# Tiles that matmuls read at multiples of 128 bytes, and the first u tiles loaded over half of h, in a hybrid attention block

## The chip, the cores and the metric

The kernel runs on one core of a Trainium2 chip. The metric is the device time in microseconds (us). All times are of single executions; the profile is one execution, taken with the hardware profiler. The engines are TensorE (PE: matmuls; PEld: its weight loads), VectorE (DVE), ScalarE (ACT), GpSimd (POOL) and SyncE (SP). SP and POOL issue nearly all DMAs, each in the order of its own queue.

## What is computed

One decoder layer for 512 tokens of width 2048, in float32, with three gated branches:

```
h    = rms_norm(x) * g                                    # 512 x 2048
proj = h @ w_in                                           # 2048 x 13712, split into the parts below
A: indexer scores -> causal top-128 of the keys -> grouped-query attention with a relative-position bias
B: latent attention (low-rank q and kv, rotary part), causal and dense, 8 heads
C: cross-attention into 256 memory tokens, 4 heads (k, v = rms_norm(mem) @ w_mem_kv)
u_n  = o_n * silu(z_n)                    for n in A, B, C      # 512 x 1024 each
y    = sum_n sigmoid(gate_n) * (u_n @ w_branch[n])              # 512 x 2048
out  = x + y @ w_out
```

## The kernel before

**Precision and matmuls.** Every large product runs as three matmuls. Each operand is split into a high and a low half (`split`, L257): ACT rounds the high half, DVE subtracts to get the low half. High times high and the two cross products are added up in PSUM. Weights become the tiles `whi` and `wlo`, h becomes `hh0..hh3` and `hl0..hl3` (four tiles of four 128-row blocks each), the gated branch outputs become `u`. Most matmuls have 512 columns.

**The weight stream.** `stream` (L310) is one list of chunks that PE follows in order. SP loads weights in pieces of 256 x 512 into `wraw` (three buffers, `NRAW`) and `sraw`; each is split two to three jobs ahead (`LOOK`), and a piece is loaded as soon as the splitting of an older one has freed its buffer. A job of a plain chunk is two 128-row blocks: 2 x 4 x 3 matmuls with 512 columns, or 12 in a job of Strassen's scheme. The order of the chunks:
1. the memory tokens' k and v;
2. the index queries;
3. Strassen products (`strassen_chunk`, L1495) for the queries of C, the latents and the gates: here weights stream over h, or over the sums `hS1, hS2, hS4` of quarters of h;
4. the rest of the input projection, among it the gated chunks (`gated_chunk`, L796), in which h streams over the weights;
5. `branch_chunk` (L1623), three times four, weights over u, in the order C, B, A;
6. `out_chunk` (L1692), weights over the merged rows `mh, ml`.

**Threads.** The attentions, norms and transposes are generators beside that stream. `run` (L510) steps a thread when a planner (`Plan`, L73) believes its inputs ready: the planner keeps a clock for each engine from fixed prices, 0.422 ns a column plus 11 ns for such a matmul. The order on each engine is so written out when the kernel is built. A thread can also wait for a flag that another part sets. Every instruction passes through `Plan.call` (L139), so nearly all rows of the profile carry L139, and groups are told apart by their tiles.

**How u is loaded.** The last gated chunk is the second half of branch B. Its `post` is `close_h` (L1761): the pool of h is closed, the pool `bp` is opened in its place on the right side of the memory, and the flag "z end" is set. `u_thread` (L1585) waits for that flag, then takes the four u tiles of branch C from `bp` (they lie where hh0, hl0, hh1 and hl1 lay) and loads them from DRAM by GpSimd's queue. In that queue they stand behind the stores of the last gated halves (`sp_u<-zo`, `sp_u<-zs`), which wait for PE, ACT and DVE. The u tiles of branch B follow one by one, each after its tile's last use by branch C ("u2 out k"); those of branch A are made on the core.

**Where tiles start.** `Slots` (L153) hands out tiles from pools; a tile takes its size rounded up to 32 bytes per partition, one after the other. Pools on the left grow upward. The first tile, `ident`, starts at 4,224 = 33 x 128. The constants' pool `cp` then holds 5,280 = 41 x 128 + 32 bytes, so the next pool, `wp` with wraw, whi and wlo, starts at 9,504, which is 32 above a multiple of 128. The other left pools carry that 32 on: memory tokens, hS, the latents, `mh`, `ml`, and most tiles of branch B's attention. The right side ends at 229,344 = 1,791 x 128 + 96, so h, u, yg and ym start 96 above a multiple. In between small tiles shift it: branch C's halves (`c_qh`, `c_kh`, `c_ph`) start at 96, branch A's `a_kh`, `a0_qh` at 64, and the bf16 table `tab` of branch A (93,568) at 0. `mnegb` (bf16, 6,048) starts at 32. `ident` at 0 is the moving operand of the transposes.

The functions of the diff and what calls them:

Of the kernel before, what the change touches and what calls it, by code (L numbers as in the profile page):

```python
# [10 lines left out]
F32 = mybir.dt.float32  # L11
F32R = mybir.dt.float32r
BF = mybir.dt.bfloat16
# [7 lines left out]
P = 128  # L21
T = 512
# [26 lines left out]
    return c  # L49


PE = object()
PRODUCTS = ("P1", "P2", "P3", "P4", "P5", "P6", "P7")


class Engine:
# [3 lines left out]
    def __init__(self, plan, eng, kind):  # L60
        self._plan, self._eng, self._kind = plan, eng, kind
# [11 lines left out]
class Plan:  # L73
# [72 lines left out]
    def ready(self, waits, slack, slack_pe):  # L146

        t = max([x.next_free() if isinstance(x, Ring) else self.done(x.tensor.name, self.wrote)
                 for x in waits if x is not PE], default=0.0)
        return t + (slack_pe if any(x is PE or isinstance(x, Ring) for x in waits) else slack)  # L150


class Slots:  # L153


    def __init__(self, plan, pool):
        self.plan, self.pool, self.past = plan, pool, {}

    def free(self, tag, n):
        past = self.past.get(tag, ())  # L160
# [3 lines left out]

    def tile(self, shape, dt, name, tag=None, bufs=1):
        tag = tag or name
        t = self.pool.tile(shape, dt, name=name, tag=tag, bufs=bufs)
        self.plan.read[t.tensor.name] = {"slot": self.free(tag, bufs)}
        self.past.setdefault(tag, []).append(t.tensor.name)
        return t  # L170
# [60 lines left out]
class Kern:  # L231
# [6 lines left out]


    @contextmanager  # L240
    def slots(self, name, **k):
        with self.tc.tile_pool(name=name, bufs=1, **k) as p:
            yield Slots(self.plan, p)

    def rsqrt(self, pool, y, v, n):

# [316 lines left out]
    def setup(self):  # L563
        nc, A = self.nc, self.A
        cp = self.cp
        jp = self.wp.tile([P, 2, 512], I32, name="jp", tag="ev", bufs=4)[:, 0, :P]
        nc.gpsimd.iota(jp, pattern=[[1, P]], base=0, channel_multiplier=-1)
        self.ident = cp.tile([P, P], F32, name="ident")
        warm = cp.tile([P, 1], F32, name="warm")
        nc.vector.memset(warm, 0.0)  # L570
        nc.scalar.activation(warm, warm, AF.Copy)
        nc.vector.tensor_scalar(self.ident, jp, 0.0, None, op0=OP.is_equal)
        self.identb = cp.tile([P, P], BF, name="identb")
        nc.vector.tensor_scalar(self.identb, jp, 0.0, None, op0=OP.is_equal)
        self.mneg = cp.tile([P, P], F32, name="mneg")
        nc.vector.tensor_scalar(self.mneg, jp, 0.0, NEG, op0=OP.is_gt, op1=OP.mult)
        self.mlow = cp.tile([P, P], F32, name="mlow")
        nc.vector.tensor_scalar(self.mlow, jp, 0.0, LOW, op0=OP.is_gt, op1=OP.mult)
        self.mnegb = cp.tile([P, P], BF, name="mnegb")
        nc.vector.tensor_copy(self.mnegb, self.mneg)  # L580
# [215 lines left out]
    def gated_chunk(self, n, c):  # L796

        nc = self.nc
        dt = self.sp["u%d%d" % (n, c)] = self.dp.tile([P, 2, 4, 512], F32, name="sp_u")
        key = "ABC"[n]  # L800
        box = {}
        new = lambda name: self.wp.tile([P, 2, 512], F32, name=name, tag="ev", bufs=4)

        def act(k):
            if k == 8:
                box["o"] = [new("zo") for _ in range(2)]
                for h, o in enumerate(box["o"]):
                    nc.gpsimd.dma_start(o, self.sp["o%s%d" % (key, c)][:, 2 * h:2 * h + 2])
            return self.act_h(k)

        def evac(b, p):
            if b % 2 == 0:
                box["s"] = new("zs")
            st, o = box["s"], box["o"][b // 2]
            s = st[:, b % 2]
            nc.scalar.activation(s, p, AF.Tanh, scale=0.5)
            nc.vector.scalar_tensor_tensor(s, s, 1.0, p, op0=OP.add, op1=OP.mult)
            if b % 2 == 0:
                return

            def gated():
                nc.vector.scalar_tensor_tensor(st, st, 0.5, o, op0=OP.mult, op1=OP.mult)

            def halves():
                h, l = o.bitcast(F32R), st.bitcast(F32R)
                self.split(h, l, st)
                nc.gpsimd.dma_start(dt[:, 0, b - 1:b + 1], o)
                nc.gpsimd.dma_start(dt[:, 1, b - 1:b + 1], st)
            self.defer(gated, False, 2)
            self.defer(halves, b == 3, 1)  # L830
        col = (AZ, BZ, CZ)[n] + c * 512
        self.chunk(self.A["w_in"][0, :, col:col + 512], KT, 512, act, "fm", 4, evac,
                   lambda k: (key if n != 1 or c else "B heads") if k == 8 else None)

# [747 lines left out]
                            lambda i, j: self.sp[keys[j]][:, 2 * i:2 * i + 2], None, done)  # L1582


    def u_thread(self):  # L1585

        nc = self.nc
        self.u = {}
        yield "z end"
        for n in (2, 1):  # L1590
            self.u[n] = []
            for k in range(4):
                if n == 1:
                    yield "u2 out %d" % k
                u = self.bp.tile([P, 2, 2, 512], F32R, name="u", tag="u", bufs=4)
                self.u[n].append(u)
                c, b = divmod(2 * k, 4)
                nc.gpsimd.dma_start(u.bitcast(F32), self.sp["u%d%d" % (n, c)][:, :, b:b + 2])
                self.flags.add("u%d%d" % (n, k))
        yield "A"  # L1600

        def load(k):
            s, o = [self.bp.tile([P, 2, 512], F32, name="u_" + x, tag="so", bufs=4) for x in "so"]
            c, b = divmod(2 * k, 4)
            nc.gpsimd.dma_start(s, self.sp["s0%d" % c][:, b:b + 2])
            nc.gpsimd.dma_start(o, self.sp["oA%d" % c][:, b:b + 2])
            return s, o
        ahead = [load(0), load(1)]
        self.u[0] = []
        for k in range(4):  # L1610
            s, o = ahead.pop(0)
            yield [s, o]
            nc.vector.scalar_tensor_tensor(s, s, 0.5, o, op0=OP.mult, op1=OP.mult)
            yield "u1 out %d" % k
            u = self.bp.tile([P, 2, 2, 512], F32R, name="u", tag="u", bufs=4)
            self.u[0].append(u)
            yield [s]
            self.split(u[:, 0], u[:, 1], s)
            if k < 2:
                ahead.append(load(k + 2))  # L1620
            self.flags.add("u0%d" % k)
# [93 lines left out]
    def build(self):  # L1715
        ctx, tc, A = self.ctx, self.tc, self.A
        self.flags, self.sp, self.chunks, self.later, self.kept = set(), {}, [], [], []
        self.turn = 0
        pool = lambda n, **k: ctx.enter_context(self.slots(n, **k))
        self.cp = pool("cp")  # L1720
        self.wp = pool("wp")
        hpool = ExitStack()
        self.hp = hpool.enter_context(self.slots("hp", side="right"))
        self.dp = pool("dp", space=DRAM)
        self.pg = Ring(self.plan, ctx.enter_context(tc.tile_pool(name="pg", bufs=4, space=PSUM)), "pg", 4)
        banks = ctx.enter_context(ExitStack())
# [32 lines left out]
            self.flags.add("gates")  # L1759

        def close_h():  # L1761
            hpool.close()
            self.bp = bpool.enter_context(self.slots("bp", side="right", reuse_waits="tile"))
            self.flags.add("z end")

# [10 lines left out]
        self.b_ss = self.cp.tile([P, 8, 8], F32, name="b_ss")  # L1776
        self.c_ss = self.cp.tile([P, 4, 6], F32, name="c_ss")
        self.l_ss = self.cp.tile([P, 3, NT], F32, name="l_ss")
        self.h = [[self.hp.tile([P, 4, T], F32R, name="h%s%d" % (x, q)) for x in "hl"] for q in range(4)]
        self.act_h = lambda k: tuple(x[:, k % 4] for x in self.h[k // 4])  # L1780
        win = A["w_in"][0]
        spool = ExitStack()
# [103 lines left out]
            self.a_bias_thread(), self.a_thread(0), self.a_thread(1), self.h_ops_thread(), self.u_thread()])  # L1886
        tpool.close()
        bpool.close()


@with_exitstack
# [23 lines left out]
```

## Time and profile before

| | us |
|---|---|
| median of 3 runs | 1927.47 (1923.93 to 1927.51) |
| the profiled execution | 1927.66 |
| its span, first to last instruction | 1925.9 |
| PE busy in it | 1887.0 |
| DVE busy | 1315.7 |
| ACT busy | 821.3 |
| POOL busy | 196.3 |

The share of the 16 DMA engines' time is 34.5% for SP's queue and 18.2% for GpSimd's; HBM is read and written at 169 GB/s over the span. The granted clock of PE is 0.995 in the mean.

How to read it: a row of a group is "engine operation out<-moving,stationary, shapes, count | busy us, mean ns of one | idle time before, and what ended it". Matmuls overlap: one lasts some 390 ns from its start to its modelled end, but the next one starts after some 230. The cost of a matmul is therefore read from one start to the next, in the timeline, and not from its duration. Columns of the timeline are start (us from the span's start), length, engine and instruction.

### The profile page before, as it was taken

The page shows a single profiled execution, that of the slowest core. Times are in us where ns is not written, and L with a number is a line of the kernel's source. Part 1 is how long each engine was busy: PE and PEld are TensorE (multiplying, and loading weights), DVE is VectorE, ACT ScalarE, POOL GpSimd, SP SyncE. Part 2 cuts the span into 40 slices and gives each one's busy share as a digit, 9 for nine tenths or more (in the row PEclk, how much of TensorE's full clock was granted, in tenths as well). Part 3 has the DMA queues.
Part 4 walks back from the last instruction along what each step waited for, and adds up shares of the span by engine and source line. Part 5 has one row for each costly group of instructions (what it writes and reads, how often), then busy time and mean ns, then how long its engine had stood idle before and what let it go on. Part 6 is the DMA issues. An engine that isn't in the chain of part 4 may idle for free.

```text
span 1925.9 us, 24974 instructions
## 1 busy us (share of the span) xinstructions
PE 1887.0 (98%) x9437; PEld 1564.0 (81%) x9437; DVE 1315.7 (68%) x2064; ACT 821.3 (43%) x1369; POOL 196.3 (10%) x308
## 2 busy tenths in 40 slices
PE   8999999999999999999999999999969999999999
PEld 6789888888888888889888888788758888778887
DVE  5676877877778768665668799975768965543232
ACT  6643554544444444447666644343323333222111
POOL 1000000000000000112110111002022222110000
PEclk9999999999999999999999999999979999999999
DMA  8754555555555556546643454335465566753442
GB/s 265 245 167 146 162 175 153 171 169 164 164 155 174 165 154 205 170 147 214 211 143 98 150 170 145 112 110 163 135 213 178 193 238 222 274 180 126 143 140 79
DMA packets 142953, 326.82 MB, mean 170 GB/s; under 512 B 13728, under 2 KB 18736, under 8 KB 142576
## 3 DMA queue, kind: packets, MB, share of 16 engines
q1 hardware_dynamic: 108176, 203.58, 34.5%
q0 software_dynamic: 34624, 121.63, 18.2%
q8 instruction: 74, 1.21, 0.3%
q14 instruction: 47, 0.39, 0.1%
q10 hardware_dynamic: 32, 0.01, 0.0%
HBM read 262.49 MB, written 62.69 MB: 169 GB/s over the span
## 4 chain that ended last, share of the span: by engine, by line
PE 92%; DVE 4%; DMA 2%; ACT 1%; issue 1%; POOL 0%; ACTq 0%; DVEq 0%; POOLq 0%
PE pg L139 58%; PE pn L139 24%; PE pb L139 3%; PE pa L139 3%; PE ra L139 2%; DVE wlo L139 1%; PE rb L139 1%; DMA wraw<-w_mem_kv 1%; ACT whi L139 1%; DVE m L139 0%; DMA u<-sp_u 0%; ACT junk L139 0%; DVE yg L139 0%; DVE i_wk L139 0%; DVE i_mx L139 0%
## 5 line engine op out<-in xcount | busy, mean ns | idle before, releaser
L139 DVE TENSOR_TENSOR wlo<-wraw,whi 128x1024 fp32r<-128x1024 f32 (+2 forms) x293 | 354.4, 1210 | 333.6 <-ACT whi L139 330.6
L139 ACT ACTIVATE whi<-wraw 128x1024 fp32r<-128x1024 f32 (+2 forms) x293 | 306.6, 1047 | 527.6 <-PE pg L139 249.1
L139 PE MATMUL pg<-whi,u 128*128 128x512 f32 x640 | 220.3, 404 | 18.7 <-DMA u<-sp_u 17.8
L139 PE MATMUL pg<-hh,whi 128*128 128x512 f32 x512 | 208.3, 407 | 2.0 <-DVE stage L139 1.3
L139 PE MATMUL pg<-hh,wlo 128*128 128x512 f32 x512 | 202.2, 395 | 0.0
L139 PE MATMUL pg<-hl,whi 128*128 128x512 f32 x512 | 202.0, 395 | 0.0
L139 PEld LDWEIGHTS pg<-whi,u 128*128 128x128 f32 x640 | 121.4, 190 | 43.7 <-issue 19.5
L139 PE MATMUL pg<-whi,hh 128*128 128x512 f32 x384 | 152.7, 398 | 0.0
L139 PE MATMUL pg<-wlo,hh 128*128 128x512 f32 x384 | 150.9, 393 | 0.0
L139 PE MATMUL pg<-whi,hl 128*128 128x512 f32 x384 | 149.7, 390 | 0.0
L139 DVE TENSOR_TENSOR wlo<-sraw,whi 128x1024 fp32r<-128x1024 f32 x79 | 96.6, 1225 | 54.4 <-ACT whi L139 54.2
L139 ACT ACTIVATE whi<-sraw 128x1024 fp32r<-128x1024 f32 x79 | 83.4, 1058 | 106.8 <-DVE sraw L139 41.2
L139 PE MATMUL pg<-wlo,u 128*128 128x512 f32 x320 | 126.1, 394 | 0.0
L139 PE MATMUL pn<-whi,hS 128*128 128x512 f32 x384 | 126.0, 389 | 0.0
L139 PE MATMUL pg<-whi,hS 128*128 128x512 f32 x384 | 126.0, 389 | 0.0
L139 PE MATMUL pn<-wlo,hh 128*128 128x512 f32 (+1 forms) x320 | 122.7, 383 | 0.0
L139 PE MATMUL pn<-whi,hh 128*128 128x512 f32 (+1 forms) x320 | 122.4, 383 | 0.0
L139 PE MATMUL pn<-whi,hl 128*128 128x512 f32 (+1 forms) x320 | 121.1, 378 | 0.0
L139 PEld LDWEIGHTS pg<-hh,whi 128*128 128x128 f32 x512 | 96.3, 188 | 23.4 <-DVE stage L139 2.2
L139 PEld LDWEIGHTS pg<-hh,wlo 128*128 128x128 f32 x512 | 96.1, 188 | 23.3
L139 PEld LDWEIGHTS pg<-hl,whi 128*128 128x128 f32 x512 | 96.4, 188 | 19.2
L139 DVE TENSOR_TENSOR wlo<-T,whi 128x1024 fp32r<-128x1024 f32 x64 | 78.2, 1222 | 36.0 <-ACT whi L139 35.8
(422 smaller groups left out, 3888.7 us busy)
## 6 DMA issues: line engine op xcount, KB each, us to landing
wraw<-w_in SPq DMA_DIRECT2D x161, 512.0 KB, 3.7
sraw<-w_in SPq DMA_DIRECT2D x79, 512.0 KB, 3.7
wraw<-w_branch SPq DMA_DIRECT2D x48, 512.0 KB, 4.2
wraw<-w_mem_kv SPq DMA_DIRECT2D x32, 512.0 KB, 5.2
wraw<-w_out SPq DMA_DIRECT2D x32, 512.0 KB, 3.7
yg<-sp_g POOLq DMA_DIRECT2D x24, 512.0 KB, 6.1
u<-sp_u POOLq DMA_DIRECT2D x8, 1024.0 KB, 7.7
sp_m<-yg POOLq DMA_DIRECT2D x16, 512.0 KB, 4.8
```

The costliest lines, as they stand in the source:

```text
L139: return f(*a, **k)
```

## The change

There are two parts.

**Alignment.** `Slots` gets a `line` of 128 bytes, for all pools but those of PSUM, DRAM and the constants. When a tag is taken for the first time, its size (rounded up to 32, times its buffers) is filled up to a multiple of 128 by a pad tile that nothing uses. In `cp`, a tile `rest` of 96 bytes after `ident` moves what follows to the next multiple of 128 for the tiles identb, mnegb and the end of the pool. On the right, a tile `edge` of 96 bytes makes h and what follows it start at a multiple.

**The loads of u.** h is held in two pools, the first for its tiles of blocks 0 to 7 and the second for blocks 8 to 15. Only the second is closed by `close_h`; `bp` opens in its place. The u tiles are taken from the first pool under the tags of hh0, hl0, hh1 and hl1, so that each waits for the readers of that tile only. The flag that starts them, "z half", is set in the last gated chunk before its block 8, that is when its first half has been issued. The four loads of branch C are issued by SP in place of GpSimd; those of branch B stay on GpSimd. The first pool is closed at the end of the kernel.

```diff
 class Slots:
-    def __init__(self, plan, pool):
-        self.plan, self.pool, self.past = plan, pool, {}
+    def __init__(self, plan, pool, line=0):
+        self.plan, self.pool, self.past, self.line = plan, pool, {}, line
...
     def tile(self, shape, dt, name, tag=None, bufs=1):
         tag = tag or name
+        new = tag not in self.past
         t = self.pool.tile(shape, dt, name=name, tag=tag, bufs=bufs)
+        if new and self.line:
+            size = math.prod(shape[1:]) * (2 if dt == BF else 4)
+            rest = -((size + 31) // 32 * 32 * bufs) % self.line
+            if rest:
+                self.pool.tile([P, rest // 4], F32, name="pad_" + tag, tag="pad_" + tag, bufs=1)
...
-    def slots(self, name, **k):
+    def slots(self, name, line=LINE, **k):
         with self.tc.tile_pool(name=name, bufs=1, **k) as p:
-            yield Slots(self.plan, p)
+            yield Slots(self.plan, p, 0 if "space" in k else line)
...
         self.ident = cp.tile([P, P], F32, name="ident")
+        cp.tile([P, 24], F32, name="rest")
...
         def act(k):
+            if k == 8 and n == 1 and c == 1:
+                self.flags.add("z half")
             if k == 8:
...
+    def u_tile(self, k):
+        u = self.hp[0].tile([P, 4, T], F32R, name="u", tag="h%s%d" % ("hl"[k % 2], k // 2))
+        return u.rearrange("p (x k) t -> p x k t", x=2)
...
-        yield "z end"
+        yield "z half"
         for n in (2, 1):
...
-                u = self.bp.tile([P, 2, 2, 512], F32R, name="u", tag="u", bufs=4)
+                u = self.u_tile(k)
...
-                nc.gpsimd.dma_start(u.bitcast(F32), self.sp["u%d%d" % (n, c)][:, :, b:b + 2])
+                (nc.sync if n == 2 else nc.gpsimd).dma_start(u.bitcast(F32), self.sp["u%d%d" % (n, c)][:, :, b:b + 2])
...
-        self.cp = pool("cp")
+        self.cp = pool("cp", line=0)
...
-        hpool = ExitStack()
-        self.hp = hpool.enter_context(self.slots("hp", side="right"))
+        hpool, hpool2 = ExitStack(), ExitStack()
+        edge = ctx.enter_context(self.tc.tile_pool(name="edge", bufs=1, side="right"))
+        edge.tile([P, (LINE - 32) // 4], F32, name="edge")
+        self.hp = [hpool.enter_context(self.slots("hp", side="right")),
+                   hpool2.enter_context(self.slots("hp2", side="right"))]
...
         def close_h():
-            hpool.close()
+            hpool2.close()
             self.bp = bpool.enter_context(self.slots("bp", side="right", reuse_waits="tile"))
             self.flags.add("z end")
...
-        self.h = [[self.hp.tile([P, 4, T], F32R, name="h%s%d" % (x, q)) for x in "hl"] for q in range(4)]
+        self.h = [[self.hp[q // 2].tile([P, 4, T], F32R, name="h%s%d" % (x, q)) for x in "hl"] for q in range(4)]
...
         bpool.close()
+        hpool.close()
```

The u tiles of branch A use `u_tile` in the same way.

More of the change, by code (lines that the diff above doesn't have):

```diff
@@ L49, in constants @@
     return c
+LINE = 128
 PE = object()
@@ L1614, in u_thread @@
             yield "u1 out %d" % k
-            u = self.bp.tile([P, 2, 2, 512], F32R, name="u", tag="u", bufs=4)
+            u = self.u_tile(k)
             self.u[0].append(u)
```

## The prediction

> **What bounds the kernel now.** I read the page first, then who waited for whom, then the rows of TensorE (PE) by shape, and last the PE timeline in a few quiet stretches.
>
> ```profile
> span 1925.9 us, 24974 instructions
> PE 1887.0 (98%) x9437; PEld 1564.0 (81%) x9437; DVE 1315.7 (68%) x2064; ACT 821.3 (43%) x1369; POOL 196.3 (10%) x308
> ```
>
> PE is busy for 98% of the span, so the end moves with two things: the time from one matmul to the next, and the waits of PE. The longest waits are:
>
> ```profile
> PE pg L139 <- DMA u<-sp_u: 17.8, 1, 17.8
> PE pb L139 <- DMA g_rows<-mem_norm_g: 4.6, 1, 4.6
> PE pg L139 <- DVE wlo L139: 2.3, 3, 0.8
> ```
>
> One wait of 17.8 us stands out: the load of u, which the change moves. Its chain, and the stretch around it (columns: PE, PEld, DVE, ACT and POOL busy, granted clock, DMA share, GB/s):
>
> ```profile
> 1398.04 0.55 POOL sp_u L139
> ...
> 1403.30 8.45 DMA u<-sp_u
> ```
> ```profile
> 14.60:110.00 95.40, 92.87 (x431) 75.42 (x432) 61.49 (x94) 61.81 (x104) 9.67 (x15) 1.00 0.75 238
> 190.00:820.00 630.00, 629.26 (x2762) 517.99 (x2761) 477.59 (x457) 297.06 (x372) 29.44 (x43) 1.00 0.54 168
> 1110.00:1270.00 160.00, 157.97 (x784) 129.40 (x783) 147.23 (x319) 66.38 (x111) 15.52 (x26) 1.00 0.43 137
> ...
> 1412.00:1419.00 7.00, 7.00 (x51) 5.49 (x52) 1.93 (x7) 0.77 (x2) 0.00 (x0) 0.61 0.89 348
> ```
>
> GpSimd first stores the four last gated halves (from 1398.04) and then issues the u loads at 1403.30; the first lands 8.45 us later. Behind the wait the granted clock is 0.61 for 7 us, against 1.00 in the stretches without a wait.
>
> Now the pace, from start to start in stretches where PE does nothing else. "Offset" is a tile's start address modulo 128, from the layout given above.
>
> ```profile
> 149.72 0.39 PE L139 MATMUL pg<-hl,whi 128*128 128x512 f32 x1
> ...
> 156.96 0.40 PE L139 MATMUL pg<-hh,wlo 128*128 128x512 f32 x1
> ...
> 701.58 0.39 PE L139 MATMUL pg<-whi,hS 128*128 128x512 f32 x1
> ...
> 704.30 0.39 PE L139 MATMUL pg<-whi,hh 128*128 128x512 f32 x1
> ...
> 709.79 0.39 PE L139 MATMUL pg<-whi,hS 128*128 128x512 f32 x1
> ...
> 1419.40 0.39 PE L139 MATMUL pg<-whi,u 128*128 128x512 f32 x1
> ...
> 1421.91 0.40 PE L139 MATMUL pg<-whi,u 128*128 128x512 f32 x1
> ...
> 1645.83 0.40 PE L139 MATMUL pn<-whi,u 128*128 128x512 f32 x1
> ...
> 1649.80 0.40 PE L139 MATMUL pn<-whi,u 128*128 128x512 f32 x1
> ```
>
> All are matmuls of 512 columns; the first name is the moving operand, the second the stationary one.
> - Both at offset 32 (weights over hS): 12 starts in 2.72 us, 226.7 ns each.
> - Moving at 32, stationary at 96 (weights over hh, hl): 24 in 5.49 us, 228.8 ns. Weights over u, the same offsets: 11 in 2.51 us (228.2 ns) and 17 in 3.97 us (233.5 ns); I take 230.9, the middle.
> - Moving at 96, stationary at 32 (h over weights): 31 in 7.24 us, 233.5 ns.
>
> So the pace goes with the offsets, though the work is the same. No wide matmul here has a moving operand at offset 0. Narrow ones do:
>
> ```profile
> L139 PE MATMUL pg<-wlo,mh 128*128 128x512 f32 x128 | 49.8, 389 | 0.0
> L139 PE MATMUL rb<-tab,a_st 128*128 128x64 bf16 x320 | 23.6, 192 | 0.0
> L139 PE MATMUL rb<-tab,a_st 128*128 128x32 bf16 x320 | 22.7, 178 | 0.0
> L139 PE MATMUL pa<-c_ph,c_vh 128*128 128x256 f32 x32 | 9.0, 282 | 0.0
> L139 PE MATMUL pb<-mnegb,identb 128*128 128x128 bf16 x32 | 7.4, 230 | 0.0
> ```
>
> The duration of one is a constant plus its columns: (389 - 282) / 256 = 0.418 ns a column. What is left is 175 ns for the two f32 rows (offsets 32 and 96) and 176.5 for mnegb (offset 32, bf16), but 165.2 and 164.6 for tab, the one operand here that starts at offset 0. So a moving operand off the 128-byte boundary costs 11.3 ns more, whatever its type. Ends are modelled, so this is a hint and no proof. It fits the pace: 512 columns at 0.418 are 214.0 ns, and 226.7 - 11.3 = 215.4.
>
> **The change part by part.**
>
> *Alignment.* It adds no instruction, only pads. All tiles that PE reads move to offset 0, so both operands have equal offsets. I price an aligned 512-column matmul at 215.4 ns; the bounds are 214.0 (columns alone) and 226.7 (equal offsets help, 0 is not special). I take 215.4 because tab is the nearest row at offset 0. The counts:
>
> ```profile
> L139 PE MATMUL pg<-hh,whi 128*128 128x512 f32 x512 | 208.3, 407 | 2.0 <-DVE stage L139 1.3 <-DVE zs L139 0.7
> L139 PE MATMUL pg<-whi,hh 128*128 128x512 f32 x384 | 152.7, 398 | 0.0
> L139 PE MATMUL pn<-whi,hh 128*128 128x512 f32 x256 | 100.4, 392 | 0.0
> L139 PE MATMUL pn<-whi,hh 128*128 128x400 f32 x64 | 22.1, 345 | 0.0
> ```
> ```profile
> 0.00:1926.00 1926.00, 1561.09 (x4928) 0.99 0.53 170
> ```
> ```profile
> 0.00:1926.00 1926.00, 961.24 (x2464) 0.99 0.53 170
> ```
> ```profile
> 0.00:1926.00 1926.00, 287.28 (x1152) 0.99 0.53 170
> ```
>
> The last three rows (PE busy with its count, clock, DMA share, GB/s) count the matmuls that read whi, wlo and u. Weights: 4928 + 2464 = 7392. Each row with hh stands for three equal ones (hi·hi and the two cross terms).
> - h over weights: 3 x 512 = 1536, x (233.5 - 215.4) = 27.8 us.
> - weights over h: 3 x (384 + 256) = 1920, x 13.4 = 25.7 us.
> - weights over u: 1152, x 15.5 = 17.9 us.
> - the 400-column ones: 3 x 64 = 192, x 11.3 = 2.2 us.
> - the rest, 7392 - 4800 = 2592 (memory tokens, hS, merged rows, latents), x 11.3 = 29.3 us.
> - the attentions' own products of 256 columns and more (c_ph above is one group of many): some 700; between 0 and 8 us, taken at 4, since short bursts among weights are often held by something else.
>
> Sum 106.9 us. The Trainium skill, "TensorE: Matmul & The Clock Gate", section "Back-to-back issue gap", gives N/2.4 + 2.5 ns, 215.7 for 512 columns; no run so far shows it, since the best pace here is 226.7. By it the sum would be some 2 us smaller.
>
> *What takes part of that back.* A faster PE needs the others to follow.
> - 1110 to 1270 us: the top-k selection keeps DVE busy for 147.2 of 160 us. PE would gain 784 x 13 ns = 10 us, down to 150, with DVE left 98% busy. Between 0 and 10 is lost; I take 6, as DVE also needs gaps.
> - 14.6 to 110 us: DMA at 0.75 share, 238 GB/s, feeds the first weights; of 431 x 11.3 ns = 4.9 us I give back 3 (0 to 4.9).
> - 190 to 820 us: DVE 477.6 of 630 us; PE would need about 597. Covered, nothing lost.
> - The order is written for a planner that prices such a matmul at 227 ns; a real 215 shortens every hand-over of the attention chains. 0 to 8 us, taken at 3, because none of them shows a wait now.
>
> Together 12 us back.
>
> *The u loads.* Four loads of 1 MB for branch C leave GpSimd's queue, where they stood behind four stores, and go to SP at the middle of the last gated chunk. The tiles they overwrite are the first half of h, read for the last time before this row:
>
> ```profile
> 1365.12 0.39 PE L139 MATMUL pg<-hh,whi 128*128 128x512 f32 x1
> ...
> 1393.70 0.39 PE L139 MATMUL pg<-hh,wlo 128*128 128x512 f32 x1
> ```
> ```profile
> u<-sp_u POOLq DMA_DIRECT2D x8, 1024.0 KB, 7.7
> ```
>
> From 1365.12 the chunk has 96 of its 192 matmuls left, 28.6 us. Now four loads begin at 1403.30; at the 348 GB/s of the 1412-to-1419 row 4.2 MB take 12 us. So they land some 16 us before they are needed. The 17.8 us go, and with them the low clock: (1 - 0.61) x 7 = 2.7 us. What is late next is the eviction of the chunk's first bank, which runs while its last matmuls do; at most 0.7 us (the zs wait in the hh row above). On SP the wait for PE holds the weight loads queued behind it. Three buffers and two to three split tiles stand ahead of PE then, some 5 jobs of 24 matmuls (28 us at 233.5 ns); the loads behind are late by at most the 12 us. I cost that at 0; without the cover it is 12 us. The loads of branch B stay on GpSimd. Gain 20.5 us.
>
> *Sum.* The profiled execution took 1927.66 us (span 1925.9), 0.2 above the median of 1927.47. 1927.7 - 106.9 + 12 - 20.5 = 1812.3 us. Own range of this case: 1796 (nothing given back, 8 us from the attentions) to 1839 (all 22.9 us of the bounds given back, nothing from the attentions, 12 us on SP).
>
> **The rivals.**
>
> *Only the mismatch is cured.* The 11 ns may belong to 4-byte operands at any offset; then everything runs at 226.7. For it: 226.7 is rigid, and a plain constant explains every width too. Against: mnegb is bf16 and has the 11 ns. Gain 1536 x 6.8 + 1920 x 2.1 + 1152 x 4.2 = 19.3 us, plus 20.5, less 1 for the selection: 1889 us.
>
> *Offsets are not the cause.* The differences could come from which buffers the streams share with other engines' traffic. Then only the u loads count: 1907 us. The Trainium skill, "Advanced Engine Details and Errata", section "Memory Cachelines", gives SBUF lines of 16 bytes; by it 32 and 96 are as good as 0, and this case would hold. The trace speaks against it: 226.7 and 233.5 ns at offsets that are both multiples of 16.
>
> *Slower.* Equal offsets at 0 might be the bad phase: a weight load and a moving read that start on the same line of the same bank. Place: every wide matmul. Price: the slowest pace seen, 233.5, against 229.4 now (the mean of the groups above), over 7200 of them: 29.5 us lost, 20.5 won, 1937 us. It decides from 232.2 ns on. Against: equal offsets at 32 are the fastest of all.
>
> That tiles stay unaligned can be ruled out by adding: the left pools begin 96 bytes higher, at 9,600 = 75 x 128, the right end is 229,248 = 1,791 x 128, and each new tag is padded to 128.
>
> **How the numbers follow.** A measurement of this kernel tells 0.2%, some 4 us, from no change. Forecast (1812): 0.62. Only the mismatch (1889): 0.20. Only the u loads (1907): 0.09. Slower (1937): 0.05. A cancellation within 0.2%: 0.04. So faster 0.91, same 0.04, slower 0.05. The range goes from 1796 to 1892: it holds nearly all of the forecast and of the first rival, about 0.8.
>
> **What would show it.** Weights over hS fall from 226.7 to 215.4 ns from start to start, and h over weights to the same pace; durations at 512 columns fall from 389 to about 378. No u wait in PE's list, no low clock near 1394, u on SP. DVE over 95% busy in the selection, with new PE waits for wlo there. If the pace stops at 226 to 227 in all groups, the step "215.4" is wrong; if the groups still differ, the offsets are not the cause; if PE waits for wlo just before the first branch chunk, SP's queue was held too long.

## The result and the profile after

| | median, us | ratio to before [95% interval] |
|---|---|---|
| before | 1927.49 (1923.93 to 1927.79) | 1 |
| after | 1894.14 (1893.69 to 1894.73) | 0.9831 [0.9814, 0.9848] |

The change saves 33 us, 1.7%. The forecast was 115 us; the measured time lies just above the range, and 5 us from the rival "only the mismatch is cured" (1889). The profiled execution took 1894.73 us.

The first two lines of the page of after, busy time by engine:

```profile
span 1892.9 us, 24971 instructions
PE 1871.0 (99%) x9437; PEld 1561.9 (83%) x9437; DVE 1315.6 (70%) x2064; ACT 820.7 (43%) x1369; POOL 193.5 (10%) x304
```

PE still bounds the kernel. Its busy time has fallen by 16 us and the span by 33, so half of the gain was idle time. The longest waits of PE after (us in total, times, longest):

```profile
PE pb L140 <- DMA g_rows<-mem_norm_g: 4.5, 1, 4.5
PE pn L140 <- DVE m L140: 2.2, 6, 0.8
PE pg L140 <- DVE wlo L140: 2.2, 3, 0.8
```

The 17.8 us for u are gone, and no wait has come in their place. SP's queue shows why (start, length, what it issued):

```profile
1349.98 7.91 SPq L140 DMA_DIRECT2D wraw<-w_branch  x2
1358.07 2.83 SPq L140 DMA_DIRECT2D u<-sp_u  x4
1364.08 34.03 SPq L140 DMA_DIRECT2D wraw<-w_branch  x6
```

The four loads leave at 1358.07, some 25 us before the first matmul needs them. On PE's timeline the last gated matmul and the first of the branch then follow each other without a gap:

```profile
1383.46 0.39 PE L140 MATMUL pg<-hh,wlo 128*128 128x512 f32 x1
1383.69 0.39 PE L140 MATMUL pg<-whi,u 128*128 128x512 f32 x1
```

The granted clock there, and the load of the engines in three other stretches (columns as in the prediction):

```profile
190.00:820.00 630.00, 629.26 (x2777) 520.70 (x2776) 481.88 (x468) 297.78 (x372) 29.44 (x43) 1.00 0.55 170
820.00:1110.00 290.00, 289.29 (x1588) 251.91 (x1587) 199.50 (x419) 183.28 (x473) 43.60 (x67) 1.00 0.49 156
1110.00:1270.00 160.00, 157.55 (x790) 130.76 (x789) 148.91 (x319) 67.59 (x112) 15.52 (x26) 1.00 0.44 139
1383.00:1392.00 9.00, 9.00 (x55) 7.36 (x54) 7.69 (x9) 5.53 (x10) 1.64 (x3) 1.00 0.35 106
```

The clock behind the hand-over is 1.00 where it was 0.61. DVE is 93% busy in the selection (148.91 of 160), not the 98% that a faster PE would have brought. Now the pace, in the longest quiet stretches of PE's timeline: 108 starts of h over weights, then 36 of weights over h.

```profile
1296.68 0.39 PE L140 MATMUL pg<-hh,whi 128*128 128x512 f32 x1
...
1320.94 0.39 PE L140 MATMUL pg<-hh,wlo 128*128 128x512 f32 x1
```
```profile
232.42 0.39 PE L140 MATMUL pn<-whi,hh 128*128 128x512 f32 x1
...
240.35 0.39 PE L140 MATMUL pn<-whi,hl 128*128 128x512 f32 x1
```

24.26 us / 107 = 226.7 ns and 7.93 / 35 = 226.6 ns, against 233.5 and 228.8 before. In such stretches all groups have come to the pace that weights over hS had, and none is faster. Aligned operands do not run at 215.4 ns. The groups (busy us, mean ns of one) say the same of the hint behind that number:

```profile
L140 PE MATMUL pg<-hh,whi 128*128 128x512 f32 x512 | 206.4, 403 | 2.5 <-DVE stage L140 1.7 <-DVE zs L140 0.8
L140 PE MATMUL rb<-tab,a_st 128*128 128x64 bf16 x320 | 23.3, 191 | 0.0
L140 PE MATMUL pb<-mnegb,identb 128*128 128x128 bf16 x32 | 7.4, 230 | 0.0
```

`mnegb` now starts at a multiple of 128 and still takes 230 ns by the profile. The 11 ns by which it stood above `tab` were not its offset.

### The profile page after: what moved, and what is told of

Same layout as the page of the kernel before. It is cut to its first block, busy times and chain, and to the rows that moved or that the text cites. A ratio compares the mean times of both kernels' runs of the same rounds, so it can differ in the third digit from the quotient of the medians.

```text
span 1892.9 us, 24971 instructions
## 1 busy us (share of the span) xinstructions
PE 1871.0 (99%) x9437; PEld 1561.9 (83%) x9437; DVE 1315.6 (70%) x2064; ACT 820.7 (43%) x1369; POOL 193.5 (10%) x304
## 4 chain that ended last, share of the span: by engine, by line
PE 90%; DVE 4%; DMA 3%; ACT 1%; issue 1%; POOL 0%; SPq 0%; ACTq 0%; DVEq 0%; POOLq 0%
PE pg L140 57%; PE pn L140 23%; PE pb L140 3%; PE pa L140 3%; PE ra L140 2%; DVE wlo L140 1%; DMA wraw<-w_mem_kv 1%; DMA ym<-sp_m 1%; PE rb L140 1%; ACT whi L140 1%; DVE m L140 0%; DVE yg L140 0%; ACT junk L140 0%; DMA u_o<-sp_oA 0%; DMA px<-mem 0%
```

## The experiments

The theories, as the expectations use them. A: equal start addresses of the two operands make the wide matmuls faster, and the wait for u is a separate 20 us. B: the addresses do nothing. C: the wait for u shrinks by itself once the rest is faster. D: what counts for u is which queue loads it, not when. E: 0 modulo 128 itself counts, not equality. F: a period of 64 bytes. G: a period longer than 128 bytes, which the change meets by chance.

### The two parts alone

**e_align** keeps the alignment and starts the loads as before:

```diff
-            if k == 8 and n == 1 and c == 1:
-                self.flags.add("z half")
...
-        yield "z half"
+        yield "z end"
...
-                (nc.sync if n == 2 else nc.gpsimd).dma_start(u...
+                nc.gpsimd.dma_start(u...
```

> The changed kernel with the u loads put back to where they were: started by the flag at the end of the last gated chunk and issued by GpSimd; all tiles stay at multiples of 128. Theory A (what counts is that moving and stationary operand have equal offsets, and the wait for u is a separate 20 us): pace 226.7 to 229 ns in all groups, a PE wait of some 18 us for u, 1914 us (1894 + 20). Rival B (the offsets do nothing and the u loads brought all of it): 1927 us, paces as in the kernel before. Rival C (the wait for u shrinks by itself once the pace is faster): under 1905 us.

Measured: 1915.1 us, 0.9939 [0.9924, 0.9954]. The wait for u is back in PE's list:

```profile
PE pg L140 <- DMA u<-sp_u: 17.3, 1, 17.3
```

**e_uload** keeps the early loads and takes the pads away (`LINE = 0`, no `rest`, no `edge`).

> The changed kernel without any pad, so with the offsets of the kernel before (weights 32, h and u 96); only the early u loads on SP remain. Theory A: 1907 to 1909 us (1927.5 less 18 to 20), no PE wait for u, h over weights still at 233.5 ns. Rival B: 1894 us. If the two parts do not add up (their gains differ from 33 us in sum by over 4), something joins them.

Measured: 1905.46 us, 0.9887 [0.9872, 0.9902], and no wait for u. Before took 1926.86 us beside these runs: alignment alone saves 11.8 us, the loads alone 21.4, and both together 33. The parts add up. So neither B nor C holds, and the early loads are worth some 21 us at either pace.

### Queue or place

**e_half_pool** loads u at the new place, but from GpSimd; **e_end_sp** at the old place, but from SP.

```diff
-                (nc.sync if n == 2 else nc.gpsimd).dma_start(u...
+                nc.gpsimd.dma_start(u...        # e_half_pool
```
```diff
-            if k == 8 and n == 1 and c == 1:
-                self.flags.add("z half")
...
-        yield "z half"
+        yield "z end"                           # e_end_sp
```

> The changed kernel with the four u loads of branch C issued by GpSimd, still at the middle of the last gated chunk. Theory A (the earlier place in the order is what counts): 1893 to 1896 us, no PE wait for u. Rival D (the queue counts, GpSimd is held by its stores): a PE wait of 5 to 18 us for u comes back, 1900 to 1914 us.

> The changed kernel with the four u loads on SP, but started at the end of the last gated chunk. Theory A: SP does not stand behind the four stores, but the transfer itself (8.45 us to the first landing) is exposed, and some low clock with it: a PE wait of 8 to 11 us for u, 1903 to 1906 us. Rival D (the queue alone does it): 1894 us.

Measured: 1894.28 us for the place without SP (0.9828 [0.9814, 0.9843]), the same as after; 1910.9 us for SP without the place (0.9918 [0.9901, 0.9934]), with 14.1 us of waiting, more than the 8 to 11 us and 1906 us that I expected at most. The wait of e_end_sp, and its chain (start, length), which shows what I had missed:

```profile
PE pg L140 <- DMA u<-sp_u: 14.1, 1, 14.1
```
```profile
1385.16 1.22 DVE zs L140
1386.37 1.15 DVE wlo L140
...
1387.54 0.37 SPq L140
...
1388.08 9.64 DMA u<-sp_u
```

SP's queue is no free road at that place. A weight load stands at its head; it waits for the buffer that DVE frees with `wlo`, and DVE is busy with `zs`. So u leaves only at 1388.08, and takes 9.64 us. The place gives the gain; where the place is late, the queue is worth 4 us (1915.1 against 1910.9). D falls.

### Is it 0, equality, or something longer

Here h and u, or all tiles, are moved by another size of `edge` (and of `rest`). Nothing else changes.

```diff
-        cp.tile([P, 24], F32, name="rest")
+        cp.tile([P, 32], F32, name="rest")                       # e_both32 only
-        edge.tile([P, (LINE - 32) // 4], F32, name="edge")
+        edge.tile([P, (LINE - 64) // 4], F32, name="edge")       # e_both32, e_right32
+        edge.tile([P, (LINE - 96) // 4], F32, name="edge")       # e_right64
+        edge.tile([P, (2 * LINE - 32) // 4], F32, name="edge")   # e_right128
+        edge.tile([P, (3 * LINE - 32) // 4], F32, name="edge")   # e_right256
+        edge.tile([P, (LINE + 32) // 4], F32, name="edge")       # e_rightm64
                                                  # e_right96: no tile edge
```

> The changed kernel with every tile 32 bytes above a multiple of 128, on the left and on the right: equal offsets, none of them 0. Theory A (only equality counts): 1894 us, the same paces as in the changed kernel. Rival E (0 itself counts, a row off the boundary costs a further read): slower by 3 us or more, 226.7 ns no longer reached by weights over h.

> The changed kernel with h and u 64 bytes above a multiple of 128, weights at 0: the difference of the kernel before, without 32 in either. Theory A: the old paces come back, 228 to 231 ns for weights over h and u, 233 for h over weights; 1907 to 1909 us. Rival F (what costs is being off a 64-byte line, as 32 and 96 are and 0 and 64 are not): 1894 us.

> The changed kernel with h and u 32 bytes above a multiple of 128, weights at 0: half the difference of the kernel before. Theory A says that unequal offsets cost, and has no price for this difference: between 1896 and 1909 us. Rival F: as bad as before, 1907 to 1909 us. If it is 1894 us, 32 bytes of difference are free and only the larger difference costs.

> The changed kernel with h and u moved down by another 128 bytes: still multiples of 128, but the difference to the weights is an odd multiple of 128, where it was a multiple of 512 before. Theory A with a period of 128: 1894 us. Rival G (the period is 256 or 512, and the changed kernel meets it by chance): 1897 to 1912 us and a pace above 228 ns for weights over h.

> The changed kernel with h and u moved by another 256 bytes: their start differs from that of the weights by 256 modulo 512, and by 0 modulo 128 and 256. Theory G says that the pace repeats with a longer period than 128 bytes. With a period of 256 bytes this is the changed kernel again: h over weights 228.7 ns, weights over h 227.1, some 1894 us. With a period of 512 bytes it is slow as the kernel moved by 128 bytes: 230 to 233 ns, 1908 to 1917 us. I hold 512 for the likelier (0.6), since 256 is the farthest point of such a period from 0.

> The changed kernel without the tile edge: h and u start 96 bytes above the weights modulo 512. If the pace depends on how far the moving operand's start lies ahead of the stationary one's, 96 lies between 64 (229.9 ns, h over weights) and 192 (233.5 ns before), so h over weights takes 230 to 233.5 ns, weights over h (96 behind) 229 to 233.3, and the time is 1906 to 1917 us. If only the distance from a multiple of 128 counted, it would be as 32 is (233.4 and 233.1 ns, 1917 us).

> The changed kernel with h and u 64 bytes below the weights modulo 512, in place of 64 above, where h over weights took 229.9 ns and weights over h 233.3. If the signed distance from the stationary start to the moving start counts, the two change places: h over weights 233.3 ns, weights over h and over u 229.9. With 1536 matmuls 3.4 ns slower and 1920 and 1152 3.4 ns faster the time is 1914.1 + 5.2 - 10.4 = 1909 us. If it belongs to which tile streams (h or weights) and not to the sign, the paces stay and the time is 1914 us.

In each trace I took the mean time from start to start of a group's neighbouring matmuls of 512 columns. The table has the distance d, the start of h less the start of the weights, modulo 256, and these means (some 1400 gaps of h over weights, 1860 of weights over h; gaps over 300 ns left out). The distance follows from the layout. Before, 9,504 is 32 and 229,344 is 224 modulo 256, so d = 192, or -64. After, 9,600 and 229,248 are both 128, so d = 0.

| kernel | d | h over weights, ns | weights over h, ns | median, us | ratio [95%] |
|---|---|---|---|---|---|
| after | 0 | 228.7 | 227.1 | 1894.14 | 0.9831 [0.9814, 0.9848] |
| e_both32 | 0, all at another start | 228.6 | 227.2 | 1893.25 | 0.9821 [0.9806, 0.9836] |
| e_right256 | 0 (moved by 256) | 228.7 | 227.1 | 1893.3 | 0.9824 [0.981, 0.9839] |
| e_right32 | 32 | 233.4 | 233.1 | 1917.24 | 0.9943 [0.9929, 0.9958] |
| e_right64 | 64 | 229.9 | 233.3 | 1914.11 | 0.9929 [0.9915, 0.9944] |
| e_right96 | 96 | 233.9 | 234.0 | 1919.9 | 0.9963 [0.995, 0.9976] |
| e_right128 | 128 | 233.0 | 232.8 | 1916.59 | 0.994 [0.9924, 0.9957] |
| e_rightm64 | -64 | 233.6 | 229.1 | 1905.5 | 0.9889 [0.9873, 0.9906] |
| e_uload | -64, as before | 233.6 | 229.1 | 1905.46 | 0.9887 [0.9872, 0.9902] |

- e_both32: with all starts 32 bytes above, nothing is lost. 0 is not special; equality is. E falls.
- e_right32 and e_right64: a mismatch alone loses 20 to 23 us. A holds in its first half, and F falls. A group that moving h doesn't shift stays where it was: weights over the merged rows, both in left pools, take 226.8 ns in after and in all six runs in which only h and u moved.
- e_right128 is the surprise: all tiles still start at multiples of 128 bytes, and the gain of the alignment is gone, with more. The quiet stretch of 97 starts of h over weights in its timeline:

```profile
1317.63 0.40 PE L140 MATMUL pg<-hh,wlo 128*128 128x512 f32 x1
...
1340.04 0.39 PE L140 MATMUL pg<-hh,wlo 128*128 128x512 f32 x1
```

22.41 us / 96 = 233.4 ns, the pace of before. So what the change says of itself, multiples of 128, isn't what helps. I held a period of 512 for the likelier (0.6); e_right256 is as fast as after, so the period is 256 bytes. G holds: that left and right pools now agree modulo 256 is luck. With one more pad of 128 bytes on one side they wouldn't.
- e_rightm64 tells whether the sign counts. Its timeline has 104 starts of h over weights and 36 of weights over h:

```profile
1296.76 0.39 PE L140 MATMUL pg<-hh,wlo 128*128 128x512 f32 x1
...
1320.79 0.40 PE L140 MATMUL pg<-hh,whi 128*128 128x512 f32 x1
```
```profile
233.34 0.39 PE L140 MATMUL pn<-whi,hh 128*128 128x512 f32 x1
...
241.36 0.39 PE L140 MATMUL pn<-whi,hl 128*128 128x512 f32 x1
```

24.03 us / 103 = 233.3 ns and 8.02 / 35 = 229.1 ns. Against e_right64 the two groups have changed places, so the sign counts: a moving operand 64 bytes ahead of the stationary one takes some 229 to 230 ns, one 64 behind 233. These are also the paces and the time of e_uload, whose starts are others but whose distance is the same modulo 256.

These runs tell the theories apart, but most of their sizes I forecast too small. I had taken e_right64 for the distance of the kernel before and expected its paces and 1907 to 1909 us. Its sign is the opposite one: the two groups' paces were the other way round, and it took 1914.11. e_right32 (expected at 1909 at most), e_right128 (1912) and e_right96 (1917) were slower than expected too.

### Where the 215 ns are

**e_bf16** uses 2-byte halves (bf16) in place of 4-byte ones in the output projection, at the same addresses:

```diff
+            if jb["c"].get("bf"):
+                h, l = h.bitcast(BF)[:, :, :512], l.bitcast(BF)[:, :, :512]
             self.split(h[:, :, :w], l[:, :, :w], src)
...
-                self.mh = self.tp.tile([P, KT, 512], F32R, name="mh")
+                self.mh = self.tp.tile([P, KT, 512], F32R, name="mh").bitcast(BF)[:, :, :512]
```

and so for `ml`, with `bf=True` for the chunks of the output projection.

> The changed kernel, but in the output projection both halves of the merged rows and of the weights are bf16 in place of f32, at the same starts (so that part is computed at a lower precision). It has 768 matmuls of 512 columns, now at 226.8 ns. If the 11 to 12 ns beyond 214 ns belong to 4-byte operands, these matmuls fall to 214 to 216 ns and the time to some 1886 us. If they belong to every matmul of 512 columns, whatever its type, the pace stays at 226.8 ns and the time at 1894 us.

Measured: 1886.5 us, 0.979 [0.9775, 0.9804]. The timeline has 113 starts between these rows:

```profile
1741.67 0.38 PE L140 MATMUL pn<-wlo,mh 128*128 128x512 bf16 x1
...
1765.85 0.38 PE L140 MATMUL pg<-whi,ml 128*128 128x512 bf16 x1
```

24.18 us / 112 = 215.9 ns, where the f32 halves took 226.8. The 11 ns belong to the 4-byte type; both operands changed together, so which of the two it is was not tested. The Trainium skill, "TensorE: Matmul & The Clock Gate", section "Back-to-back issue gap", gives N/2.4 + 2.5 ns as the gap of an isolated matmul, by estimate 215.8 ns for 512 columns: this trace agrees for bf16 operands, and disagrees by 11 ns for the 4-byte operands of this kernel. For a sustained stream of weight loads and matmuls the same section of the Trainium skill gives some 131 ns at 512 columns; no run here shows that.

**e_bf_all** does that to all products with weights, by a `bitcast` of `whi`, `wlo`, `hh`, `hl`, `hS1` to `hS4`, `u`, `mh`, `ml`, the latents and the memory tokens; the quarters of h that go out to DRAM and back (`a21`) are then bf16 too. **e_bf_off** is the same without the tile `edge`, so with d = 96.

```diff
-        edge = ctx.enter_context(self.tc.tile_pool(name="edge", bufs=1, side="right"))
-        edge.tile([P, (LINE - 32) // 4], F32, name="edge")
```

> The changed kernel, but all products with weights (memory tokens, h, the sums of h, latents, u, merged rows) have both halves of both operands in bf16 in place of f32, at the same starts; these products are so computed at a lower precision, and the planner prices them at 0.417 ns a column plus 1 ns. The question is whether the rest of the prediction's sum stands once the matmuls do run at the 215.4 ns that it took for granted. 7392 matmuls go from some 227.5 to 215.9 ns, about 11.6 ns each, 86 us: 1808 us if nothing is given back. With the 12 us that the prediction gave back (selection 6, first weights 3, attention chains 3) 1820 us; with the most that it allowed, 22.9 us, 1831 us. If bf16 gains only in the output projection, where little else runs, it is 1870 us or more.

> The kernel of e_bf_all (all products with weights in bf16 halves, at a lower precision) without the tile edge, so that h and u start 96 bytes above the weights modulo 256. With f32 halves that cost 1919.9 - 1894.1 = 26 us (234 ns in place of 227 to 229). If the dependence on the distance of the starts belongs to 4-byte operands only, the time equals that of e_bf_all within 0.3%. If it belongs to the reads of both tiles whatever their type, it is some 20 to 26 us above e_bf_all; if half the bytes are half the trouble, some 10 to 13 us above.

Measured: 1836.9 us (0.9535 [0.9519, 0.9552]) and 1836.91 us (0.9535 [0.9521, 0.9549]). With bf16 halves the distance of 96 bytes, worth 26 us with f32, costs nothing: the dependence belongs to the 4-byte operands. And the fast pace isn't all gain: of 86 us only 57 arrive. The waits of e_bf_all, and its chain of waits before the longest:

```profile
PE pn L140 <- ACT u L140: 9.4, 1, 9.4
PE pg L140 <- DVE stage L140: 7.9, 7, 2.2
PE pg L140 <- DVE wlo L140: 3.6, 5, 0.9
PE ra L140 <- DVE a_q L140: 3.4, 1, 3.4
PE ra L140 <- DVE bm L140: 2.6, 1, 2.6
```
```profile
1548.67 7.85 PE ra L140 x40
...
1558.53 4.88 DMA u_o<-sp_oA
...
1564.77 1.06 ACT u L140
...
1567.14 3.17 PE pn L140 x7
```
```profile
1320.00:1566.00 246.00, 227.96 (x1650) 136.27 (x1680) 200.95 (x471) 84.76 (x160) 54.34 (x81) 0.98 0.61 207
```

The weights overtake branch A's attention. Its last products (`ra`) have PE to themselves from 1548.67; then its output must be stored, loaded again (4.88 us) and split before branch A can begin. In that stage, 1320 to 1566 us, PE is idle for 18 us, 15.4 of them in the three waits for `a_q`, `bm` and `u`. The wait has a second price: the granted clock around it is 0.53 (columns as in the prediction).

```profile
1561.00:1572.00 11.00, 5.47 (x13) 1.90 (x15) 4.81 (x4) 2.11 (x2) 2.37 (x5) 0.53 0.82 274
```

## Why the prediction was wrong

**The step that failed is "I price an aligned 512-column matmul at 215.4 ns".** It came from modelled durations of narrow matmuls: `tab`, at offset 0, had 11 ns less than `mnegb`, at offset 32. The profile after has `mnegb` at a multiple of 128 with the same 230 ns. The aligned matmul measured 226.7 ns, at best. The pace that the step needed appears in none of the address experiments, and at once with bf16 halves (215.9). The rival had it right: "the 11 ns may belong to 4-byte operands at any offset". I argued against it with `mnegb` being bf16, a duration whose end is modelled. A sentence of the kernel itself spoke for it: its planner has two prices, of which I had looked at the second alone.

```python
if aps[1].dtype == BF:
    return 0.417 * n + 1
return max(0.422 * n + 11, 109) if n >= 128 else 214
```

Point by point:

- **Alignment, -106.9 us forecast.** Measured -11.8 alone. The rival's own sum for the pace was 19.3. From the means over the traces it is 1536 x 4.9 + 1920 x 2.0 + 1152 x 1.9 ns = 13.5 us (weights over u 230.3 before, 228.4 after). The rest of the 19.3 is missing because the rival let every matmul fall to 226.7. That holds in quiet stretches. Where the attention's short products run between (1588 PE instructions in the 290 us from 820 to 1110, 5.5 a us, against 4.4 in the stretch before), weights over h keep a mean of some 229 ns, against 226.7 in the stretch from 190 to 820 us. The trace of after shows why: behind anything else on PE the pace takes some ten matmuls to settle. An example behind four transposes:

```profile
1125.80 0.60 PE L140 MATMUL pb<-ident,b_kv 128*128 128x128 f32 x4
...
1126.47 0.40 PE L140 MATMUL pg<-hl,whi 128*128 128x512 f32 x1
...
1128.78 0.39 PE L140 MATMUL pg<-hh,wlo 128*128 128x512 f32 x1
...
1132.18 0.39 PE L140 MATMUL pg<-hh,wlo 128*128 128x512 f32 x1
```

  Ten gaps from 1126.47 on take 2.31 us, 231 ns each; the fifteen after them 3.40 us, 226.7 ns. Over the whole trace h over weights takes 230.3 ns in the first twelve gaps of a run without other PE work (749 gaps, those over 300 ns left out) and 226.7 from the thirteenth on (625). With bf16 halves (e_bf_all) the two means are 216.2 and 215.8. The same shows without other work between: weights over hS, whose distance e_right64 doesn't change, stand there directly behind weights over h at 233 ns. Their first six gaps take 231.5 ns in the mean, and 226.7 from the seventh on; in after they take 226.7 to 226.9 from the first. So with 4-byte operands the first matmuls of a run still carry something of what ran before them. Why is open.
- **Weights over u, 230.9 ns.** The prediction's two rows, 228.2 and 233.5 ns, have the same offsets, which a pace that goes with the offsets alone doesn't allow; I took the middle and passed over that. In the trace of before the 233.3 ns hold from just behind a short wait (1623.37) to the transposes at 1671.03, and on either side of it the same group takes some 229 to 230. e_uload and e_rightm64, at the same distance, have no such stretch (229.5 in the mean). So the distance doesn't fix the pace alone; what interrupted PE last counts too. That 230.9 is near the mean of 230.3 is luck.
- **What is given back, +12 us.** In after hardly anything had to be given back: no wait of PE has grown by more than 1 us. In e_bf_all, where the pace did come, 1808 forecast without it became 1836.9: 29 us, more than the 22.9 that I took for the most. The selection (6) was not the place: PE's listed waits there come to 4.4 us (1080 to 1240 us), against 2.5 in after (1110 to 1270 us). The chains of branch A's attention, put at 3 because none of them showed a wait, were: 9.4 us for `u`, and 6.0 for `a_q` and `bm`. No wait in the old profile only meant that the slack was not yet used up. And PE ran at a low clock around its waits (0.53, 0.51 and 0.72 in 1561 to 1572, 1548 to 1555 and 949 to 955 us, where after has 1.00): that costs some 7 us, an estimate from PE's busy time and the missing clock in these three stretches. The prediction had priced the low clock for the wait for u alone, and none for new waits. The planner's order is another in that kernel, as it prices bf16 differently; part of the 29 may belong to that.
- **The loads of u, -20.5 us.** Right: 21.4 alone, 21.0 on top of the alignment. Both of its parts show in the profile, the wait gone and the clock at 1.00 behind the hand-over.
- **SP's queue, 0 us.** Right: with GpSimd as the issuer the time is the same. No wait for `wlo` has come up before the first branch chunk, which fits the cover of weights split ahead.
- **"Offsets are not the cause" (1907 us).** Wrong; e_uload is that case at 1905.46, and after is 11 us faster. The Trainium skill, "Advanced Engine Details and Errata", section "Memory Cachelines", has lines of 16 bytes; all distances here are multiples of 16, and the pace goes from 227 to 234 ns with them, so no run here bears out that only such lines count.
- **"Slower" (1937 us): equal offsets as the bad phase.** Wrong; equality is the good phase, at any common start that was tried.
- **The layout.** "Offset" modulo 128 was the wrong measure. The forecast asked only that all tiles reach a multiple of 128; e_right128 meets that too and takes 1916.59 us.

## What to carry over

Take the price of a matmul from start to start, in a group of the same type and width; a modelled duration of another shape is not a second witness. With 4-byte operands look at the distance of the two start addresses modulo 256, not at either of them: between 0 and a bad distance lie 26 us of 1894 here, and a pad added on one side can throw them away. When two rows of the same group disagree, look for what differs before taking their middle. Before pricing a faster bound engine, look for the chain that has just enough slack now; it will show no wait in the old profile.

The fastest kernel that ran is e_bf_all, 1836.9 us, at the lower precision of bf16 halves; with f32 halves nothing tried is faster than after by more than 1 us.

## What the runs showed of the hardware

- In this kernel the pace of 512-column matmuls with 4-byte operands depends on the start of the moving less the start of the stationary operand, modulo 256: 226.7 ns at 0, about 229 to 230 at +64 (but 233.3 in one stretch of before), and 233 to 234 at -64, 32, 96 and 128 on either side. It is no matter of more distance, more time, and it has a sign. Why is open.
- That pace has to settle behind other work on PE, or behind matmuls at another distance: 230.3 ns in the first twelve gaps and 226.7 after them, for h over weights in after; 231.5 in the first six and 226.7 after them, for weights over hS in e_right64.
- bf16 operands show none of it, and their pace is 215.9 ns. A difference that may bear on it, from the groups of weight loads of after and of e_bf_all (mean ns of one behind the busy time):

```profile
L140 PEld LDWEIGHTS pg<-hh,whi 128*128 128x128 f32 x512 | 96.4, 188 | 21.8 <-DVE stage L140 2.6
```
```profile
L140 PEld LDWEIGHTS <-hh 128*128 128x128 bf16 x1408 | 136.1, 98 | 157.2 <-issue 6.8
```

A 4-byte weight load takes 188 ns of the 227 that the matmul beside it leaves, a bf16 one 98 of 216. That the two reads get into each other's way for 4-byte operands would fit, and wasn't tested; the shown length of this group's weight loads doesn't tell, since it is 188 ns in before, in after, in e_right32, e_right64 and e_right96, and 189 in e_right128.
